# Two convolution channels summed in one PSUM bank, and a new order of the steps: a one-core diffusion layer

## The chip, the cores and the metric

The kernel runs on one core of a Trainium2 chip. The metric is the time of one execution on the device in microseconds (us); it comes as the median of several runs. One execution more is taken with a hardware profiler: its trace shows what each engine did and when. The engines are TensorE (PE; PEld is its weight load), VectorE (DVE), ScalarE (ACT), GpSimd (POOL) and SyncE (SP), which issues nearly all the transfers. Each runs its own instructions in the order in which they were written, and waits for the others by semaphores. SBUF is the large memory on the chip, PSUM the small one of eight banks into which TensorE writes.

## What is computed

One layer over 256 latent tokens of width 1024, with 256 context tokens, all in 32-bit floats. Cut to what matters here:

```python
mod   = silu(c) @ w_ada + b_ada                   # shifts, scales and gates, 6 x 1024 columns
z     = modulate(rms_norm(x)) @ w_in              # 2048 columns; for the context too
u     = z[:, :512] * sigmoid(z[:, 512:1024])      # 4 blocks of 128 channels ("ct")
u     = dwconv(u, conv_dw, 31 taps) + conv_b      # along rows of 64 tokens, each channel by itself
conv  = silu(layer_norm(u) * ln_g + ln_b)
lru   = scan(forward) + scan(backward)            # gated linear recurrence of z[:, 1024:1536]
lru   = lru * gelu(z[:, 1536:])
x     = x + g1 * (concat(conv, lru) @ w_out)
h     = modulate(rms_norm(x))
y     = top-1-group / top-2-expert mixture of 32 experts, (silu(h @ w1) * (h @ w3)) @ w2
out   = rms_norm(x + g2 * y) * final_g
```

The weights of the 32 experts are 12 MB each and are read whole; they make up most of the 443 MB that come from HBM.

## The kernel before

**Two parts.** The prelude computes all up to the router's choice of experts. The expert part (lines 826 and on) then runs expert by expert: `up` (line 828) loads a weight matrix in four tiles of 1 MB and multiplies each as it arrives. All weights go through a pool of 19 buffers of 1 MB (`slot()`, line 76). A buffer comes free when its last reader is done, and SP issues the transfers in program order, so a load waits until there is a buffer, and all loads behind it with it. PSUM tiles (`bank()`, line 73) come out of a pool of eight in the same way.

**The order of the prelude.** Up to line 345 it is written out: norm, modulation, and the projection for value and gate of the convolution (`vgproj`) in four stages of the contraction. The rest is the string `ORDER` (lines 30 to 40), a list of steps by one letter (line 807), each with its indices. The program's instructions are written in just this order; so it sets each engine's queue, and SP's and POOL's too. The steps that matter here:

- `v`, `l`: last stage of the value and gate projection, and the gating into a padded buffer `cbs[ct]` (lines 316 and 428). `glu` takes a tanh on ScalarE and a product on VectorE.
- `t` (`vtap`, line 444): a tap of the convolution on VectorE. It takes y = x * w + y with x a shifted view of `cbs[ct]` and y a quarter of `ypre`, both in SBUF, 256 columns; the first tap of a channel block (line 448) sets y, the other 30 (line 450) are chained. `VTAPS` gives 31 taps to VectorE for ct 0 and ct 3, none for ct 1, nine for ct 2, 71 in all.
- `s` and `i` (`stap`, line 452): the other 53 taps, of ct 1 and ct 2. The product x * w is made on ScalarE (`s`, line 467) or VectorE (`i`, line 465) into a ring of four buffers, and POOL adds it (line 468).
- `h`, `o`: the weights of the recurrent branch come in two buffers. Each is split into a rounded part (a cast, `split_hi`, line 287) and a rest (a subtract, `split_lo`, line 293), so that a product can be made of three passes in the format float32r. `HI` and `LO` name the engines: V, S or G (VectorE, ScalarE, POOL).
- `u`, `c`: the product of the recurrent branch for one block (line 361, 24 matmuls; the first half needs the first buffer's split alone), and its short convolution, one pass on ScalarE and three on VectorE that read the PSUM bank (lines 372 and 376).
- `p`, `a`, `d`, `q`, `n`: gate products into two banks (line 382), their activations on ScalarE with one square on the engine that `SQ` names (line 390), two products on VectorE (410, 411), a square root (414) and the scans (416).
- `b`: one of 16 steps of the modulation's remaining columns; it loads 1 MB and multiplies it (line 478). `z`, `e`: the gelu branch. `L`, `I`, `J`: load an output weight and split it; only the pair of blocks that `OS` marks is split, and `WH`, `WL`, `MH`, `ML` name the engines.
- `M`, `C`, `Q`, `R`, `N`: the layer norm of the convolution. `M` sums the four blocks on TensorE (line 558), and VectorE reads the mean (line 560).
- `X`, `O`, `D` and on: the output product, the residual, the second norm, the router and the gathering of tokens for the first experts.

Of the kernel before, what the change touches and what calls it, by code (L numbers as in the profile page):

```python
# [16 lines left out]
T = 256  # L17
# [10 lines left out]


ORDER = """  # L30
v0 h0 h1 o0 v1 l0 v3 o1 v2 t l1 l3 u1 i t*3 s u0 t*2 b t*2 s t b s t i l2 i t s*4 t*5 s t s t*3 i*2 t*3 s t*3 i
s*2 c1 t i t*2 b t b s i s*2 t*3 c0 b s*2 u2 t s*2 c2 i p10 p00 a10 i t a00 u3 p11 t i t i s t*3 p20 b p01 t i
t*2 s t d10 s i c3 t*2 i p30 t i s t b s i t*2 a20 i a30 t b r1 w t p21 t*2 s d00 a01 t i b t*2 s q10 d30 i t
d20 t i t*2 i*2 b*2 q20 s q30 t*4 i t q00 n00 z0 t z1 s p31 d01 L2 t*3 s L0 a21 t n20 a11 b k1 a31 I0 M C2 z2
n10 C1 C0 I2 C3 L4 b d21 d11 b d31 q21 q11 q01 Q b*2 R n01 z3 N1 N0 L6 e0 N2 N3 X3 X1 n30 n21 n11 X0 m0 J0 O001
e3 I4 X2 J2 O110 J4 O100 e1 q31 O011 O111 O112 x O000 e2 g I6 O003 X4 O012 n31 m3 O010 J6 m1 X5 O101 m2 X7 X6 r2
O105 O015 O002 O102 O103 O005 O007 O013 O006 O004 O016 O106 O113 O107 j k2 O017 O014 y O114 O104 O115 D00 D01
H00 Y0 O116 D10 O117 H01 H10 D11 K00 H11 B K01 Z0 K10 T0 K11 P0 F0 G02 G00 G06 G04 Y1 G05 T1 Z1 G07 P1 F1 G03 G01
G10 G11 G12 G16 G14 A1 U0 G15 U1 G17 G13 U2 U3 A0 U4 U7 U6 U5
"""  # L40
VTAPS = (31, 0, 9, 31)
SIDE = (1, 2,)
HI, LO = "VS", "VG"
SQ = ("SSSG", "SSSG")
LNSQ = "SGGG"
XC = ("SS", "SV")
WH, WL = "SSVS", "VGVV"
MH, ML = "GSSGGSVS", "GVGGGVVG"
GL = ("GG", "GG")
OS = "0010"  # L50


COLS = {}
# [9 lines left out]
def hybrid_layer(ctx: ExitStack, tc: tile.TileContext, sp_d, x_d, c_d, bada_d, rb_d, fg_d, gw_d,  # L63
# [103 lines left out]
    def first_norm(s, src):  # L167
        for t in range(2):
            S.activation(xn[:, 1], src[:, t], AF.Square, accum_out=sums[:, 2 * s + t:2 * s + t + 1])
        rstd_t = rsqrt_pow(sums[:, 2 * s:2 * s + 2], 2, 1.0 / D)  # L170
        for t in range(2):
            V.tensor_scalar(diag[:, 2 * s + t], ident, rstd_t[:, t:t + 1], None, OP.mult)
        for k2 in range(4):
            pt = bank()
            for i in range(4):
                k, t = k2 * 2 + i // 2, i % 2
                P.matmul(pt[:, i * 128:(i + 1) * 128], src[:, t, k * 128:(k + 1) * 128], diag[:, 2 * s + t],
                         start=True, stop=True)
            (V.tensor_copy, S.copy)[s](xs[s][:, k2 * 2:k2 * 2 + 2], pt.rearrange("p (k t) -> p k t", k=2))

    first_norm(0, x1)

# [104 lines left out]
    def split_hi(w, hi, lo, en):  # L287
        if en is S:
            S.copy(hi, w)  # L289
        else:  # L290
            en.tensor_copy(hi, w)

    def split_lo(w, hi, lo, en):
        en.tensor_tensor(lo, w, f(hi), OP.subtract)  # L294
# [31 lines left out]
    def prepare(q):  # L326
        ada_h(q, pt)
        for k in range(2 * q, 2 * q + 2):
            modulated(k)

    w = load_wz(0)
    split_hi(*w, S)
    split_lo(*w, G)
    prepare(0)
    for q in range(4):
        ks = range(2 * q, 2 * q + 2)
        if q < 3:
            w = load_wz(q + 1)
            rows = ada_rows(ada_first(q + 1))
            split_hi(*w, S)  # L340
            split_lo(*w, G)
            vgproj(0, ks)
            pt = ada_turn(rows)
            prepare(q + 1)
            for ct in range(1, 4):
                vgproj(ct, ks)
# [88 lines left out]
    def rows4(a):  # L435
        return a.rearrange("p (r t) -> p r t", r=4)

    vtaps = [(ct, j) for ct in range(4) for j in range(VTAPS[ct])]  # L440
    staps = [(ct, j) for ct in SIDE for j in range(VTAPS[ct], 31)]
    nring = [0]

    def vtap():
        ct, j = vtaps.pop(0)
        y, x, w = rows4(ypre[:, ct]), cbs[ct][:, :, j:j + 64], dwh[:, j * 4 + ct:j * 4 + ct + 1]
        if j == 0:
            V.tensor_scalar(y, x, w, col("convb", ct), OP.mult, OP.add)
        else:
            V.scalar_tensor_tensor(y, x, w, y, OP.mult, OP.add)  # L450

    def stap(vec=False):
        ct, j = staps.pop(0)
        n = VTAPS[ct]
        y, x, w = rows4(ypre[:, ct]), cbs[ct][:, :, j:j + 64], dwh[:, j * 4 + ct:j * 4 + ct + 1]
        acc = rows4(g2bc[:, 752:1008]) if n else y
        if j == 0:
            S.activation(acc, x, AF.Identity, scale=w, bias=col("convb", ct))
        elif j == n:
            S.mul(acc, x, w)  # L460
        else:
            p = rows4(fgbc[:, nring[0] % 4 * T:(nring[0] % 4 + 1) * T])
            nring[0] += 1
            if vec:
                V.tensor_scalar(p, x, w, None, OP.mult)  # L465
            else:
                S.mul(p, x, w)
            G.tensor_tensor(acc, acc, p, OP.add)  # L468
        if j == 30 and n:
            G.tensor_tensor(y, y, acc, OP.add)  # L470


    ada = {}
# [329 lines left out]
    def route(t):  # L803
        val["r", t] = topk(t)

    engines = {"V": V, "S": S, "G": G}
    steps = dict(v=lambda ct: vgproj(ct, (6, 7)), l=glu, t=vtap, s=stap, i=lambda: stap(True), u=u_mm, c=u_conv, p=gate_mm,
                 a=lambda ct, d: gate_act(ct, d, engines[SQ[d][ct]]), d=gate_v, q=root, n=scan, b=ada_step,
                 h=lambda i: split_hi(*wu[i], engines[HI[i]]), o=lambda i: split_lo(*wu[i], engines[LO[i]]),
# [376 lines left out]
```

## Time and profile before

| | us |
|---|---|
| median of 3 runs | 1161.3 (1160.74 to 1161.55) |
| the profiled execution's own time | 1162.45 |
| its span, first to last instruction | 1160.7 |
| TensorE busy in the span | 1022.5 (88%) |
| VectorE busy | 331.1 (29%) |
| ScalarE busy | 167.5 (14%) |
| POOL busy | 95.3 (8%) |
| bytes moved | 445.25 MB, a mean of 384 GB/s |

The profile gives start and length of each instruction, grouped by source line, operation and tile, and what ended a wait. Busy shares over the whole span say little here, because the prelude and the expert part have different limits; the views are read by stretches of time from the span's start.

### The profile page before, as it was taken

The page shows a single profiled execution, that of the slowest core. Times are in us where ns is not written, and L with a number is a line of the kernel's source. Part 1 is how long each engine was busy: PE and PEld are TensorE (multiplying, and loading weights), DVE is VectorE, ACT ScalarE, POOL GpSimd, SP SyncE. Part 2 cuts the span into 40 slices and gives each one's busy share as a digit, 9 for nine tenths or more (in the row PEclk, how much of TensorE's full clock was granted, in tenths as well). Part 3 has the DMA queues.
Part 4 walks back from the last instruction along what each step waited for, and adds up shares of the span by engine and source line. Part 5 has one row for each costly group of instructions (what it writes and reads, how often), then busy time and mean ns, then how long its engine had stood idle before and what let it go on. Part 6 is the DMA issues. An engine that isn't in the chain of part 4 may idle for free.

```text
span 1160.7 us, 12269 instructions
## 1 busy us (share of the span) xinstructions
PE 1022.5 (88%) x4923; PEld 425.1 (37%) x4923; DVE 331.1 (29%) x644; ACT 167.5 (14%) x313; POOL 95.3 (8%) x105
## 2 busy tenths in 40 slices
PE   7897899899999998988888888888888888888796
PEld 6763456443434232323232323232323222232234
DVE  4899993412121112111211111212121111111113
ACT  3436762300101000000000000000000000000002
POOL 2455522000000000000000000000000000000001
PEclk9898898899999999999999999999999999999999
DMA  9856869498999999999999999999999999999995
GB/s 346 300 195 240 327 262 389 183 423 348 420 419 420 421 420 419 419 420 420 420 420 421 419 419 420 419 420 419 420 419 420 420 420 419 419 420 420 419 393 190
DMA packets 76930, 445.25 MB, mean 384 GB/s; under 512 B 7187, under 2 KB 17475, under 8 KB 27204
## 3 DMA queue, kind: packets, MB, share of 16 engines
q1 hardware_dynamic: 76658, 443.85, 93.9%
q8 instruction: 41, 0.67, 0.2%
q10 hardware_dynamic: 210, 0.55, 0.1%
q14 instruction: 21, 0.17, 0.0%
HBM read 443.32 MB, written 1.05 MB: 383 GB/s over the span
## 4 chain that ended last, share of the span: by engine, by line
DMA 65%; PE 19%; DVE 13%; issue 1%; ACT 0%; POOL 0%; SPq 0%; DVEq 0%; ACTq 0%; POOLq 0%
DMA slot<-in_w_dram 65%; PE bank L835 12%; DVE xn L450 4%; PE bank L661 2%; PE bank L770 1%; PE bank L857 1%; DVE fgbc L465 1%; DVE slot L294 1%; PE bank L322 1%; DVE slot L376 1%; DVE slot L284 1%; DVE slot L410 1%; DVE slot L419 1%; DVE lw L209 0%; DVE slot L411 0%
## 5 line engine op out<-in xcount | busy, mean ns | idle before, releaser
L835 PE MATMUL bank<-slot 128*64 128x512 f32 x1984 | 469.4, 601 | 82.7 <-DMA slot<-in_w_dram 82.7
L835 PEld LDWEIGHTS bank<-slot 128*64 128x64 f32 x1984 | 129.4, 136 | 406.3 <-DMA slot<-in_w_dram 194.2
L835 PE MATMUL bank<-slot,gt 128*64 128x512 f32 x992 | 220.4, 596 | 3.6 <-DMA slot<-in_w_dram 2.6
L946 DVE TENSOR_TENSOR sl<-sl,bank 128x512 f32<-128x512 f32 x31 | 21.3, 687 | 491.7 <-issue 468.0
L835 PEld LDWEIGHTS bank<-slot,gt 128*64 128x64 f32 x992 | 68.1, 137 | 144.9 <-issue 133.0
L982 DVE TENSOR_TENSOR yy<-bank,g2bc 64x512 f32<-64x512 f32 x62 | 42.7, 688 | 194.6 <-PE bank L835 194.2
L939 ACT ACTIVATE sl<-bank 128x512 f32<-128x512 f32 x31 | 18.5, 597 | 456.8 <-PE bank L835 456.8
L1103 POOL TENSOR_TENSOR slot<-x,fgbc 128x256 f32<-128x256 f32 x6 | 4.2, 727 | 938.3 <-DVE x L1100 938.3
L857 PE MATMUL bank<-yy,st 128*128 128x512 f32 x120 | 58.0, 606 | 0.0
L770 PE MATMUL bank<-oh,xn 128*128 128x256 f32 x224 | 54.6, 387 | 0.0
L770 PEld LDWEIGHTS bank<-oh,xn 128*128 128x128 f32 x224 | 41.9, 197 | 14.7 <-issue 11.4
L966 ACT COPY gt<-bank 128x256 f32<-128x256 f32 x31 | 11.5, 373 | 221.4 <-DVE gt L965 221.4
L862 DVE TENSOR_TENSOR x<-x,bank 128x512 f32<-128x512 f32 x60 | 39.7, 683 | 7.1 <-PE bank L857 7.1
L776 ACT ACTIVATE slot<-bank,gsp 128x256 f32<-128x256 f32 x32 | 18.0, 564 | 152.4 <-PE bank L770 148.9
L322 PE MATMUL bank<-slot 128*128 128x256 f32 x192 | 28.8, 310 | 6.0 <-ACT slot L283 4.8
L857 PEld LDWEIGHTS bank<-yy,st 128*128 128x128 f32 x120 | 20.6, 191 | 26.5 <-issue 23.2
L322 PEld LDWEIGHTS bank<-slot 128*128 128x128 f32 x192 | 26.6, 212 | 8.1 <-ACT slot L283 5.8
L779 DVE TENSOR_SCALAR slot<-bank,gsp 128x256 f32<-128x256 f32 x32 | 17.3, 543 | 41.1 <-ACT slot L776 41.0
L294 POOL TENSOR_TENSOR slot<-slot 128x2048 fp32r<-128x2048 f32 x5 | 23.8, 4768 | 26.9 <-ACT slot L289 26.9
L450 DVE SCALAR_TENSOR_TENSOR xn<-cb,sp,xn 128x256 f32<-128x256 f32 x38 | 25.1, 662 | 0.7
L468 POOL TENSOR_TENSOR xn<-xn,fgbc 128x256 f32<-128x256 f32 x30 | 23.7, 791 | 16.6 <-DVE fgbc L465 9.6
L367 PE MATMUL bank<-slot 128*128 128x512 f32 x96 | 23.4, 400 | 1.4 <-DVE slot L294 1.4
(246 smaller groups left out, 706.7 us busy)
## 6 DMA issues: line engine op xcount, KB each, us to landing
slot<-in_w_dram SPq DMA_DIRECT2D x372, 1024.0 KB, 19.9
slot<-in_wada_dram SPq DMA_DIRECT2D x16, 1024.0 KB, 6.7
slot<-in_w_dram SPq DMA_DIRECT2D x24, 512.0 KB, 10.8
slot<-in_wada_dram SPq DMA_DIRECT2D x16, 512.0 KB, 10.8
slot<-in_win_dram SPq DMA_DIRECT2D x8, 1024.0 KB, 10.5
slot<-in_wout_dram SPq DMA_DIRECT2D x4, 1024.0 KB, 9.4
x<-in_x_dram SPq DMA_DIRECT2D x2, 512.0 KB, 4.3
slot<-in_ctx_dram SPq DMA_DIRECT2D x2, 512.0 KB, 6.6
```

Source lines behind the costliest of these rows:

```text
L294: en.tensor_tensor(lo, w, f(hi), OP.subtract)
L322: P.matmul(pvg[ct][:, i * T:(i + 1) * T], wz[k // 2][wi][:, k % 2, c:c + 128], x[k // 4][:, k % 4, 0:T], start=k + i + n == 0, stop=k == 7 ...
L367: P.matmul(pu, w, x[k // 4][:, k % 4], start=k + n == 0, stop=k == 7 and n == 2)
L450: V.scalar_tensor_tensor(y, x, w, y, OP.mult, OP.add)
L468: G.tensor_tensor(acc, acc, p, OP.add)
L661: P.matmul(p, m[:, q], w[:, c:c + 512], start=first and n == 0, stop=len(done) == 8 and n == len(passes) - 1)
L770: P.matmul(pg[:, i * 256:(i + 1) * 256], xn[:, t, pair(k)], oh[:, t].rearrange("p e s -> p (e s)"), start=t + i == 0, stop=t == 1 and i == ...
L835: P.matmul(ps[64 * h:64 * h + 64, :], xs(k2 * 2 + i), w[:, i, h * 512:(h + 1) * 512], start=k2 + i == 0, stop=k2 * 2 + i == 7, tile_positi ...
L857: P.matmul(pz, st[:, t * 128:(t + 1) * 128], yy[:, h * 512:(h + 1) * 512], start=True, stop=True)
L862: V.tensor_tensor(x1[:, t, q], x1[:, t, q], pz, OP.add)
L946: V.tensor_tensor(gg, sl, pb, OP.mult)
L982: V.tensor_tensor(yy[o:o + 64, h * 512:(h + 1) * 512], py[64 * h:64 * h + 64, :], g2bc[64 * h:64 * h + 64, h * 512:(h + 1) * 512], OP.mult)
```

## The change

Three things. The sums of the blocks ct 0 and ct 3 (`PC`) stand in the two halves of one PSUM bank, and only the last tap writes the result to `ypre` in SBUF. The string `ORDER` is a new one; with it 11 steps `i` stand where there were 24, the rest are `s`. And some splits go to other engines: both casts and both subtracts of the recurrent branch's weights (`HI`, `LO`) to ScalarE and POOL, three gate squares, and the subtract of the output weight (`WL`, third letter) to POOL. `ZH`, `ZL` and `FN` are new names for choices that were fixed.

```diff
--- before.py
+++ after.py
@@ -28,26 +28,30 @@
 
 
 ORDER = """
-v0 h0 h1 o0 v1 l0 v3 o1 v2 t l1 l3 u1 i t*3 s u0 t*2 b t*2 s t b s t i l2 i t s*4 t*5 s t s t*3 i*2 t*3 s t*3 i
-s*2 c1 t i t*2 b t b s i s*2 t*3 c0 b s*2 u2 t s*2 c2 i p10 p00 a10 i t a00 u3 p11 t i t i s t*3 p20 b p01 t i
-t*2 s t d10 s i c3 t*2 i p30 t i s t b s i t*2 a20 i a30 t b r1 w t p21 t*2 s d00 a01 t i b t*2 s q10 d30 i t
-d20 t i t*2 i*2 b*2 q20 s q30 t*4 i t q00 n00 z0 t z1 s p31 d01 L2 t*3 s L0 a21 t n20 a11 b k1 a31 I0 M C2 z2
-n10 C1 C0 I2 C3 L4 b d21 d11 b d31 q21 q11 q01 Q b*2 R n01 z3 N1 N0 L6 e0 N2 N3 X3 X1 n30 n21 n11 X0 m0 J0 O001
-e3 I4 X2 J2 O110 J4 O100 e1 q31 O011 O111 O112 x O000 e2 g I6 O003 X4 O012 n31 m3 O010 J6 m1 X5 O101 m2 X7 X6 r2
-O105 O015 O002 O102 O103 O005 O007 O013 O006 O004 O016 O106 O113 O107 j k2 O017 O014 y O114 O104 O115 D00 D01
-H00 Y0 O116 D10 O117 H01 H10 D11 K00 H11 B K01 Z0 K10 T0 K11 P0 F0 G02 G00 G06 G04 Y1 G05 T1 Z1 G07 P1 F1 G03 G01
-G10 G11 G12 G16 G14 A1 U0 G15 U1 G17 G13 U2 U3 A0 U4 U7 U6 U5
+v0 v1 h0 h1 o0 l0 t*2 v3 o1 t*3 v2 u0 l3 t*2 l1 l2 u1 t*2 b t s t s t*2 b t s t*2 s t s*3 t s*2 t s t i t s t s*2 t i
+t*2 c1 t*2 b t s*2 t*3 s*2 t s b s*3 t*2 c0 b s*2 u2 s c2 s p10 s i p00 b a10 t*2 i*3 a00 u3 t p11 t s t w i t*3 b p01
+t p20 s c3 s t s t s p30 t*2 d10 s t s*2 i t*2 a20 s*2 a30 t b t d00 t p21 a01 t r1 b t*2 s q10 t d30 i t d20 i b s b
+t*2 s L0 q30 s q20 t s t*3 q00 z0 t L4 t b z1 t i p31 t*2 n00 s t*2 n20 d01 M a11 a31 k1 I0 C2 L2 z2 n10 C1 a21 I2 C0
+C3 d21 d11 b q21 q11 q01 d31 Q z3 b R n01 e0 N1 L6 N2 x X1 N0 b X2 N3 I4 X3 b n30 n11 X0 m0 J0 J2 O001 e3 O002 J4 O100
+q31 O111 O102 O112 O000 O011 e1 O012 I6 O010 O003 g n21 n31 O110 e2 O113 J6 j m1 X5 O101 m3 m2 X4 X7 X6 r2 O103 O005
+O007 O013 O006 O105 O004 O015 O106 k2 O016 O114 O104 O017 O014 O107 D00 O115 D01 y H00 Y0 D10 O117 O116 H01 H10 D11
+K00 H11 K01 Z0 K10 K11 T0 P0 F0 G06 B G04 G02 G00 Y1 T1 G07 P1 Z1 G03 F1 G01 G05 G10 G11 G12 G16 G14 A1 U0 G17 G15 U1
+U4 G13 U2 U3 U6 U5 A0 U7
 """
 VTAPS = (31, 0, 9, 31)
+
+PC = (0, 3)
 SIDE = (1, 2,)
-HI, LO = "VS", "VG"
-SQ = ("SSSG", "SSSG")
+HI, LO = "SS", "GG"
+SQ = ("SGGG", "SSSS")
 LNSQ = "SGGG"
 XC = ("SS", "SV")
-WH, WL = "SSVS", "VGVV"
-MH, ML = "GSSGGSVS", "GVGGGVVG"
+WH, WL = "VSVS", "VVGV"
+MH, ML = "VSSGGSSG", "GVGGGVVG"
 GL = ("GG", "GG")
 OS = "0010"
+ZH, ZL = "SSSS", "GGGG"
+FN = "VS"
 
 
 COLS = {}
@@ -176,7 +180,7 @@
                 k, t = k2 * 2 + i // 2, i % 2
                 P.matmul(pt[:, i * 128:(i + 1) * 128], src[:, t, k * 128:(k + 1) * 128], diag[:, 2 * s + t],
                          start=True, stop=True)
-            (V.tensor_copy, S.copy)[s](xs[s][:, k2 * 2:k2 * 2 + 2], pt.rearrange("p (k t) -> p k t", k=2))
+            (V.tensor_copy if FN[s] == "V" else S.copy)(xs[s][:, k2 * 2:k2 * 2 + 2], pt.rearrange("p (k t) -> p k t", k=2))
 
     first_norm(0, x1)
 
@@ -328,17 +332,18 @@
         for k in range(2 * q, 2 * q + 2):
             modulated(k)
 
+    engines = {"V": V, "S": S, "G": G}
     w = load_wz(0)
-    split_hi(*w, S)
-    split_lo(*w, G)
+    split_hi(*w, engines[ZH[0]])
+    split_lo(*w, engines[ZL[0]])
     prepare(0)
     for q in range(4):
         ks = range(2 * q, 2 * q + 2)
         if q < 3:
             w = load_wz(q + 1)
             rows = ada_rows(ada_first(q + 1))
-            split_hi(*w, S)
-            split_lo(*w, G)
+            split_hi(*w, engines[ZH[q + 1]])
+            split_lo(*w, engines[ZL[q + 1]])
             vgproj(0, ks)
             pt = ada_turn(rows)
             prepare(q + 1)
@@ -437,17 +442,26 @@
 
 
 
+    yps = {}
+
+    def ypart(ct):
+        if ct not in yps:
+            b = bank()
+            for i, c in enumerate(PC):
+                yps[c] = b[:, i * T:(i + 1) * T]
+        return yps[ct]
+
     vtaps = [(ct, j) for ct in range(4) for j in range(VTAPS[ct])]
     staps = [(ct, j) for ct in SIDE for j in range(VTAPS[ct], 31)]
     nring = [0]
 
     def vtap():
         ct, j = vtaps.pop(0)
-        y, x, w = rows4(ypre[:, ct]), cbs[ct][:, :, j:j + 64], dwh[:, j * 4 + ct:j * 4 + ct + 1]
+        y, x, w = rows4(ypart(ct) if ct in PC else ypre[:, ct]), cbs[ct][:, :, j:j + 64], dwh[:, j * 4 + ct:j * 4 + ct + 1]
         if j == 0:
             V.tensor_scalar(y, x, w, col("convb", ct), OP.mult, OP.add)
         else:
-            V.scalar_tensor_tensor(y, x, w, y, OP.mult, OP.add)
+            V.scalar_tensor_tensor(rows4(ypre[:, ct]) if j == 30 else y, x, w, y, OP.mult, OP.add)
 
     def stap(vec=False):
         ct, j = staps.pop(0)
@@ -467,7 +481,7 @@
                 S.mul(p, x, w)
             G.tensor_tensor(acc, acc, p, OP.add)
         if j == 30 and n:
-            G.tensor_tensor(y, y, acc, OP.add)
+            (V.tensor_tensor(y, acc, rows4(ypart(ct)), OP.add) if ct in PC else G.tensor_tensor(y, y, acc, OP.add))
 
 
     ada = {}
@@ -803,7 +817,6 @@
     def route(t):
         val["r", t] = topk(t)
 
-    engines = {"V": V, "S": S, "G": G}
     steps = dict(v=lambda ct: vgproj(ct, (6, 7)), l=glu, t=vtap, s=stap, i=lambda: stap(True), u=u_mm, c=u_conv, p=gate_mm,
                  a=lambda ct, d: gate_act(ct, d, engines[SQ[d][ct]]), d=gate_v, q=root, n=scan, b=ada_step,
                  h=lambda i: split_hi(*wu[i], engines[HI[i]]), o=lambda i: split_lo(*wu[i], engines[LO[i]]),
```

## Rows read from the trace of the kernel before

**Rows 1.** Stretches ahead of the expert products: us, busy by engine, clock, DMA share, GB/s.
```profile
203.00:206.00 3.00, 1.46 (x6) 1.35 (x7) 2.03 (x11) 2.56 (x4) 0.94 (x2) 0.50 0.02 5
...
219.00:222.00 3.00, 3.00 (x16) 0.87 (x12) 0.44 (x2) 0.38 (x1) 0.00 (x0) 1.00 0.99 396
```

**Rows 2.** The chain of waits, 225 to 420 us: start, length, what.
```profile
381.43 19.89 DMA slot<-in_w_dram
```

**Rows 3.** The stretch of the convolution, columns as in rows 1.
```profile
69.00:145.00 76.00, 63.62 (x329) 35.49 (x328) 74.08 (x124) 46.49 (x78) 43.28 (x53) 0.91 0.62 244
```

**Rows 4.** VectorE by line and form, 60 to 175 us: busy us, mean ns.
```profile
L450 DVE SCALAR_TENSOR_TENSOR xn<-g2bc,sp,xn 128x256 f32<-128x256 f32 x30 | 19.8, 661 | 0.9
...
L465 DVE TENSOR_SCALAR fgbc<-cb,sp 128x256 f32<-128x256 f32 x12 | 5.5, 463 | 0.0
```

**Rows 5.** VectorE in order of time: start, length, instructions.
```profile
62.17 6.58 DVE L294 TENSOR_TENSOR slot<-slot 128x2048 fp32r<-128x2048 f32 x1
...
69.12 0.41 DVE L448 TENSOR_SCALAR xn<-g2bc,sp 128x256 f32<-128x256 f32 x1
...
120.60 3.40 DVE L450 SCALAR_TENSOR_TENSOR xn<-cb,sp,xn 128x256 f32<-128x256 f32 x4
...
142.80 2.04 DVE L450 SCALAR_TENSOR_TENSOR xn<-cb,sp,xn 128x256 f32<-128x256 f32 x4
...
147.75 0.41 DVE L560 TENSOR_SCALAR cb<-bank 128x256 f32<-128x256 f32 x1
...
169.04 2.29 DVE L294 TENSOR_TENSOR slot<-slot 128x2048 fp32r<-128x2048 f32 x1
```

**Rows 6.** VectorE's instructions on a PSUM bank: min/median/max ns.
```profile
L376 DVE SCALAR_TENSOR_TENSOR slot<-bank,sp,slot x12: 732/748/749, 89.7 to 113.9; 128x510 f32<-128x510 f32 x8, 128x508 f32<-128x508 f32 x4
L582 DVE TENSOR_TENSOR xn<-xn,bank x4: 411/414/415, 158.8 to 159.8; 128x256 f32<-128x256 f32 x4
```

**Rows 7.** VectorE by line and form, 189 to 197 us: the residual.
```profile
L675 DVE TENSOR_TENSOR x<-x,t 128x512 f32<-128x512 f32 x4 | 2.8, 692 | 0.1
L674 DVE TENSOR_TENSOR t<-bank,fgbc 128x512 f32<-128x512 f32 x4 | 2.8, 688 | 1.5 <-PE bank L661 1.4
```

**Rows 8.** POOL in order of time.
```profile
52.49 4.60 POOL L294 TENSOR_TENSOR slot<-slot 128x2048 fp32r<-128x2048 f32 x1 [3.33 <-ACT slot L289]
61.09 5.51 POOL L294 TENSOR_TENSOR slot<-slot 128x2048 fp32r<-128x2048 f32 x1 [4.00 <-ACT slot L289]
...
89.89 2.35 POOL L468 TENSOR_TENSOR xn<-xn,fgbc 128x256 f32<-128x256 f32 x3 [2.25 <-DVE fgbc L465]
```

**Rows 9.** ScalarE in order of time: a cast of 2048 columns.
```profile
59.12 1.89 ACT L289 CAST slot<-slot 128x2048 fp32r<-128x2048 f32 x1
```

**Rows 10.** ScalarE by line and form, 60 to 175 us: one of a gate's activations.
```profile
L398 ACT ACTIVATE slot<-t,nkh 128x512 f32<-128x512 f32 x8 | 6.5, 814 | 0.3
```

**Rows 11.** TensorE in order of time, with the wait ahead in brackets.
```profile
68.80 10.76 PE L367 MATMUL bank<-slot 128*128 128x512 f32 x46 [1.35 <-DVE slot L294]
...
109.53 3.65 PE L387 MATMUL bank<-slot 64*64 64x512 f32 x16
...
117.69 1.92 PE L492 MATMUL bank<-slot,silc 128*32 128x512 f32 x16
...
121.40 1.52 PE L486 MATMUL bank<-bada,ident 48*32 48x128 f32 x16
...
125.57 7.17 PE L306 MATMUL bank<-slot 128*128 128x256 f32 x32
...
175.68 3.03 PE L661 MATMUL bank<-slot,t 128*128 128x512 f32 x6 [2.06 <-ACT t L289]
...
214.44 7.09 PE L835 MATMUL bank<-slot 128*64 128x512 f32 x32
```

**Rows 12.** POOL by line and form, 60 to 175 us: adds of channel 2.
```profile
L468 POOL TENSOR_TENSOR g2bc<-g2bc,fgbc 128x256 f32<-128x256 f32 x21 | 17.4, 830 | 14.9 <-DVE fgbc L465 14.1
```

**Rows 13.** TensorE by line and form, 60 to 200 us: the mean product M.
```profile
L558 PE MATMUL bank<-xn,ones 128*128 128x256 f32 x8 | 4.1, 672 | 3.5 <-ACT slot L404 2.1 <-DVE xn L450 1.4
```

## The prediction

> **What bounds the kernel now.** I read the stretches of the DMA first, then the chain of waits, then the busy times by stage, then each engine in order of time inside the stage that counts.
>
> The chain of waits, as I followed it, lies on TensorE's expert products to 381 us and then goes from one weight transfer to the next [rows 2]. But already from 219 us the DMA engines are 0.99 busy [rows 1], and the products before 381 us use up what they bring. So from there the end is a fixed number of bytes at a fixed rate: it moves with the moment at which this stream starts. It starts when the first expert products hand buffers back (they begin at 214.4 us [rows 11]); just before, from 203 us on, the DMA does nothing (share 0.02, 5 GB/s) [rows 1], because all weight buffers are full and wait for the router. A prelude that is shorter by X moves the start, and so the end, by X.
>
> The prelude's middle, 69 to 145 us, is VectorE's: 74.08 of 76 us busy, against 46.5 on ScalarE and 43.3 on POOL; TensorE shows 63.6 [rows 3]. That is the stage of the 31-tap convolution. VectorE's 68 chained taps there take 0.66 us each and the 23 tap products that it makes for POOL 0.46 [rows 4]. But a tap runs in 0.51 us while POOL is idle (142.8 us, four in 2.04) and in 0.85 while POOL is busy (120.6 us, four in 3.40) [rows 5]. So a third of a tap's time is POOL in the way. After the stage a shorter one follows on VectorE; then the output products on TensorE, with one gap of 2.06 us at 175.7 us [rows 11]; then the router, which the change leaves as it is.
>
> **The change, part by part.**
>
> *Taps in PSUM (channels 0 and 3).* 60 chained taps get one SBUF operand in place of two. What the trace has of such a form is the mix-in of the short convolution (line 376: input in PSUM, sum in SBUF): 12 of them from 89.7 to 114.7 us, 732 to 749 ns [rows 6], some inside POOL's work (89.9 to 92.2 us [rows 8]), the last with POOL idle. So one SBUF operand isn't slowed by POOL. The Trainium skill says the same (SBUF — State Buffer, Who interferes with whom). No row has VectorE writing PSUM. Bounds for a tap: 0.41 us (256 columns out of PSUM, line 582) below, 0.75 us (line 376, twice the columns) above [rows 6]. I take 0.51, the same chained instruction without POOL: 60 x (0.66 - 0.51) = 9.0 us off VectorE. The ends give 15 us, and a loss of 5.
>
> *The splits of the input weights (h0, o0).* VectorE loses a cast and a subtract of 6.58 us; the same subtract takes 2.29 us at 169.0 us, where POOL is idle [rows 5]: at 62.2 us it ran against POOL's own of 5.51 us, which takes 4.60 alone [rows 8]. In the new order ScalarE casts both (1.89 each [rows 9]) before the first tanh of the gating: 59.1 + 3.8 = 62.9, and with that tanh and the first gating product (0.4 each) the first tap starts at 63.7 in place of 69.1 [rows 5]: 5.4 us. POOL subtracts both, 61.0 to 65.6 and 65.6 to 70.2. TensorE can run half of the first recurrent-branch product (u0) on the first of them; it ends that and u1 (46 instructions in 10.76 us [rows 11], so 5.6 a product) at 70.2 + 2.8 + 5.6 = 78.6, where before it ended at 79.6. Who waits is c1 on VectorE: with 25 taps and five short instructions ahead of it, it could start at 78.1 and starts at 79.4, behind ScalarE's pass over the product (512 columns, 0.8 [rows 10]): 1.3 us lost.
>
> *Tap products.* VectorE makes 10 in place of 23. 13 x 0.46 are 6.0 us, of which I take 4.9, as the records of neighbours overlap a little. ScalarE takes them at some 0.5 each (half the columns of [rows 10]), 6.5 us onto its 46.5 [rows 3], in a stage that gets to be 63: 10 us are free. POOL adds 51 products at no more than 0.83 [rows 12]: 70.2 + 42 + 3 for one more square than before is 116, ahead of the last tap. The two squares that POOL gets and the one that it gives are in this. All of it costs nothing as long as ScalarE and POOL keep that lead of about 10 us; beyond it every us counts.
>
> *New waits.* c2 waits for u2. TensorE's order is u1, five ada steps (0.96 each, their bias 1.52 [rows 11]), u2: 78.6 + 6.3 + 5.6 = 90.5, and ScalarE's pass 91.3. VectorE arrives at 79.4 + 2.3 for c1 + 3.1 for six taps in PSUM + 2.3 for three in SBUF + 2.3 for c0 = 89.4 and loses 1.9. Behind c2 on VectorE stand the rest of channel 2's taps and those of channel 3. One gate step (d01, two instructions of the length in [rows 7], 1.4) goes behind the last tap.
>
> VectorE's last tap, which ended at 144.8 [rows 5]: 5.4 + 9.0 + 4.9 + 1.4 - 1.3 - 1.9 = 17.5 earlier, 127.3.
>
> *TensorE is late next.* From u2 on: two gate pairs (1.83 each) and an ada step, 95.2; u3, 100.8; then six gate pairs 11.0, six ada steps 5.8, bias 1.5, two gelu products 7.2 (32 in 7.17) [rows 11]: 126.3 without a wait. But the sums hold one of eight PSUM banks for all that time, and gate pairs take two each until ScalarE has read them. Counted through the order, live banks reach 10 at p30 in place of 9, so p30 and the second ada bank wait for a release: bounds 0 and one gate's activations each (four or five of up to 0.81 [rows 10], so 3 us). I take 1.5 each: 129.3. The mean product M stands behind these; its eight matmuls are 4.1 us [rows 13], 133.4, and VectorE's use of it (line 560) comes 14.3 us before its 147.75 [rows 5].
>
> The strings FN, ZH, ZL and MH change no instruction: they name the engines of before, or splits that this kernel doesn't make.
>
> *After M* the steps on VectorE are the old ones in another order, and ScalarE reloads its tables once less: 0. The subtract of the fourth split (2.29 us, 169.0) leaves VectorE for POOL and runs earlier, against scans that it will slow; it stood ahead of the last scan, for which TensorE waited 2.06 us [rows 11]. Between nothing and 2.06 I take 1.0.
>
> *SP's queue.* Two loads of the output weights (L0, L4) move ahead of the twelfth ada load and L6 ahead of the last two; three of the last four ada steps stand later in TensorE's order, and their buffers, which the first expert weights get, come free later by that. The 13 us in which the DMA stands idle before the first expert product [rows 1] cover this; without them each us late would count in full.
>
> Sum: 14.3 + 1.0 = 15.3. The profiled execution took 1162.45 for a span of 1160.7; less 15.3 that is 1147.1. The median of the runs lies 1.1 lower: **1146 us**.
>
> **The rivals.**
>
> *PSUM taps cost a fixed sum more.* A chained line 376 has 0.748 us for about 510 columns [rows 6], while two 512-column rows with and without a PSUM input are equal, 688 and 692 ns (lines 674, 675) [rows 7]. The first leaves room for some 0.06 a tap, the second speaks against it: 60 x 0.06 = 3.6 less, 1150. Against the change speaks also a table of the Trainium skill (VectorE: DVE Perf Modes, the errata section), with a fixed 120 cycles for PSUM sources and 58 for SBUF. By it, an estimate, 65 ns a tap and 1150. The equal rows disagree with that. Chance 0.12.
>
> *Banks and handoffs are the new bound.* Four gate or ada steps (p30, p21, b9, p31) each wait a whole gate of activations, 3 us: 12 in place of my 3, M 9 later, 1155. For it: live banks pass eight, and TensorE is within 3 us of VectorE. Against it: ScalarE has 10 us free in the stage, so a gate that is ready is read soon. Chance 0.15.
>
> *Slower.* Writing and rereading PSUM in place costs VectorE much more. The taps' 9.0 and the 6.3 of the rest go when a tap takes 0.51 + 15.3/60 = 0.765, just past the upper bound. At the 0.85 of a hindered tap [rows 5] 20.4 us are lost against my sum: 1166. For it: no row of the form at all. Against: half the columns of line 376. Chance 0.07.
>
> *The change doesn't reach the end.* The expert weights come so much later that the DMA idles as long as before: 1161. Against it the 13 idle us. Chance 0.05.
>
> **How the numbers follow.** The forecast (14 to 20 us of VectorE time, of which TensorE lets 10 to 19 through: 1142 to 1151) has 0.61. A measurement of this kernel tells about 0.2%, 2.3 us, from no change. Faster: 0.61 + 0.12 + 0.15, so 0.88; same 0.05; slower 0.07. The range of 8 in 10 takes in the forecast, the fixed sum and most of the bank case, with the taps' lower bound below: 1139 to 1156.
>
> **What would show it.** Right: taps of channels 0 and 3 near 0.5 us whether POOL is busy or not; the first tap near 64, u1's end near 79, the last tap near 127, line 560 near 133, the first expert product 15 us earlier; DMA still idle ahead of it. Wrong: taps over 0.6 us; VectorE idle for long at c1 or c2; TensorE waiting for gate activations; no idle DMA before the first expert product, or an end that moves by less than that product does.

## The result, and the profile of the changed kernel

The changed kernel takes 1142.4 us (median of 4 runs, 1140.06 to 1145.41), the kernel before 1161.4 (4 runs): ratio 0.9838 (95%: 0.9813 to 0.9862), 19.1 us less. Two executions far off all others, one of the kernel before with 3573 us and one of e8_norm_rows_first with 2050 us, are left out of the figures. The forecast had 1146 with a range of 1139 to 1156: faster, as it said, and by about 4 us more than its sum. The profiled execution took 1141.62 for a span of 1139.8, so it lies 20.9 us below the span of before.

VectorE in the convolution, grouped by line and form (columns as in [rows 4]); lines have moved by 14, so a chained tap is line 464:

```profile
L464 DVE SCALAR_TENSOR_TENSOR bank<-g2bc,sp,bank 128x256 f32<-128x256 f32 x29 | 14.1, 488 | 0.8
L464 DVE SCALAR_TENSOR_TENSOR bank<-cb,sp,bank 128x256 f32<-128x256 f32 x29 | 14.1, 486 | 0.7
L464 DVE SCALAR_TENSOR_TENSOR xn<-cb,sp,xn 128x256 f32<-128x256 f32 x8 | 5.9, 734 | 0.2
L479 DVE TENSOR_SCALAR fgbc<-g2bc,sp 128x256 f32<-128x256 f32 x5 | 3.6, 732 | 1.2 <-POOL xn L482 1.2
L479 DVE TENSOR_SCALAR fgbc<-cb,sp 128x256 f32<-128x256 f32 x5 | 2.2, 440 | 0.0
```

A tap whose sum stands in PSUM takes 487 ns; before it took 661 [rows 4]. The eight taps of channel block 2, whose sum is still in SBUF, take 734 in the same stretch. VectorE in order of time (start, length, the wait ahead in brackets):

```profile
63.49 0.55 DVE L462 TENSOR_SCALAR bank<-g2bc,sp 128x256 f32<-128x256 f32 x1
67.95 6.78 DVE L464 SCALAR_TENSOR_TENSOR bank<-g2bc,sp,bank 128x256 f32<-128x256 f32 x13
78.31 0.92 DVE L479 TENSOR_SCALAR fgbc<-g2bc,sp 128x256 f32<-128x256 f32 x1 [0.90 <-POOL xn L482]
90.65 2.31 DVE L381 SCALAR_TENSOR_TENSOR slot<-bank,sp,slot 128x508 f32<-128x508 f32 x3 [0.85 <-ACT slot L377]
111.88 2.58 DVE L464 SCALAR_TENSOR_TENSOR bank<-cb,sp,bank 128x256 f32<-128x256 f32 x5
127.23 0.48 DVE L464 SCALAR_TENSOR_TENSOR xn<-cb,sp,bank 128x256 f32<-128x256 f32 x1
130.93 0.41 DVE L574 TENSOR_SCALAR cb<-bank 128x256 f32<-128x256 f32 x1
147.59 4.88 DVE L426 TENSOR_TENSOR_SCAN slot<-slot 128x256 f32<-128x256 f32 x1
```

The first tap is at 63.5, the last ends at 127.7, and VectorE reads the mean at 130.9; in [rows 5] these are 69.1, 144.8 and 147.75. POOL, in order of time, over the first of these taps and at their end:

```profile
60.99 9.20 POOL L298 TENSOR_TENSOR slot<-slot 128x2048 fp32r<-128x2048 f32 x2 [4.00 <-ACT slot L293]
70.15 20.46 POOL L482 TENSOR_TENSOR xn<-xn,fgbc 128x256 f32<-128x256 f32 x25
...
116.66 6.28 POOL L482 TENSOR_TENSOR g2bc<-g2bc,fgbc 128x256 f32<-128x256 f32 x7 [3.81 <-ACT fgbc L481]
...
125.28 0.99 POOL L484 TENSOR_TENSOR xn<-xn,g2bc 128x256 f32<-128x256 f32 x1
```

Thirteen taps run in 6.78 us, 0.52 each, from 67.95, first under POOL's long subtract and then under its adds, with no difference. From 112.85 to 116.66 POOL is idle; the five taps from 111.88, the last three of them in that gap, take 0.52 each as well. TensorE in order of time, the lines that answer to [rows 11] and the work before the router:

```profile
70.25 8.00 PE L372 MATMUL bank<-slot 128*128 128x512 f32 x34 [0.18 <-POOL slot L298]
108.68 1.07 PE L392 MATMUL bank<-slot 64*64 64x512 f32 x4 [1.19 <-ACT slot L409]
112.32 1.07 PE L392 MATMUL bank<-slot 64*64 64x512 f32 x4 [0.57 <-ACT slot L409]
127.77 1.99 PE L572 MATMUL bank<-xn,ones 128*128 128x256 f32 x8
137.27 5.39 PE L310 MATMUL bank<-slot 128*128 128x256 f32 x16
146.70 9.71 PE L675 MATMUL bank<-slot,xn 128*128 128x512 f32 x22
173.97 1.88 PE L675 MATMUL bank<-slot,xn 128*128 128x512 f32 x4
193.84 7.09 PE L848 MATMUL bank<-slot 128*64 128x512 f32 x32
```

The first expert product (line 848) begins 20.6 us earlier. The stretches ahead of it, as in [rows 1], still show an idle DMA, for some 9 us where it was 13:

```profile
186.00:190.00 4.00, 4.00 (x25) 3.75 (x25) 2.13 (x12) 3.06 (x6) 0.99 (x1) 0.50 0.34 137
190.00:194.00 4.00, 4.00 (x23) 3.87 (x24) 2.46 (x10) 2.28 (x6) 1.57 (x2) 0.62 0.00 0
```

**Where the 20.6 us come from**, by stages of the two traces:

| stage | before | after | gained |
|---|---|---|---|
| start to the first tap | 69.1 | 63.5 | 5.6 |
| first tap to VectorE's use of M | 78.6 | 67.4 | 11.2 |
| from there to the first output product | 14.05 | 15.8 | -1.7 |
| output products, first to last | 34.1 | 29.15 | 5.0 |
| from there to the first expert product | 18.5 | 18.0 | 0.5 |
| first expert product to the end of the span | 946.3 | 946.0 | 0.3 |

The fourth row is what the forecast missed. Output products of before, the same columns by stretches: the wait of [rows 11] and what follows it.

```profile
173.60:175.70 2.10, 0.04 (x2) 0.02 (x1) 0.09 (x2) 0.48 (x2) 1.91 (x3) 1.00 1.02 429
175.70:178.50 2.80, 2.77 (x6) 1.98 (x7) 0.45 (x1) 0.41 (x1) 0.17 (x1) 0.58 1.00 418
178.50:182.30 3.80, 3.80 (x10) 1.96 (x9) 0.00 (x0) 0.00 (x0) 0.00 (x0) 0.86 1.02 425
```

TensorE waits at 1.00 (the 2.4 GHz level), and when it goes on, the granted clock is 0.58 and then 0.86, part of the time at 1.2 GHz. By these clocks the same work at 1.00 would have been (1 - 0.58) x 2.8 + (1 - 0.86) x 3.8 = 1.7 us shorter, an estimate. The changed kernel has no such wait: the whole stretch of its output products is at 1.00.

```profile
146.70:176.00 29.30, 29.30 (x93) 15.21 (x90) 18.13 (x22) 9.88 (x19) 11.41 (x12) 1.00 1.00 413
```

### The profile page after: what moved, and what is told of

It reads as the page before. It is cut to its first block, busy times and chain, and to the rows that moved or that the text cites. A ratio compares the mean times of both kernels' runs of the same rounds, so it can differ in the third digit from the quotient of the medians.

```text
span 1139.8 us, 12269 instructions
## 1 busy us (share of the span) xinstructions
PE 1015.8 (89%) x4923; PEld 420.9 (37%) x4923; DVE 309.8 (27%) x628; ACT 172.7 (15%) x325; POOL 103.0 (9%) x108
## 4 chain that ended last, share of the span: by engine, by line
DMA 68%; PE 22%; DVE 6%; issue 1%; ACT 1%; POOL 1%; SPq 0%; DVEq 0%; ACTq 0%; POOLq 0%
DMA slot<-in_w_dram 68%; PE bank L848 11%; PE bank L675 2%; PE bank L372 2%; DVE bank L464 1%; PE bank L870 1%; PE bank L784 1%; PE bank L326 1%; PE bank L506 1%; DVE slot L288 1%; PE bank L810 1%; DVE lw L213 0%; PE bank L310 0%; DVE g1s L268 0%; POOL slot L298 0%
## 5 line engine op out<-in xcount | busy, mean ns | idle before, releaser
L848 PEld LDWEIGHTS bank<-slot,gt 128*64 128x64 f32 x992 | 68.1, 137 | 144.8 <-issue 133.0
L952 ACT ACTIVATE sl<-bank 128x512 f32<-128x512 f32 x31 | 18.5, 597 | 456.6 <-PE bank L848 456.6
L298 POOL TENSOR_TENSOR slot<-slot 128x2048 fp32r<-128x2048 f32 x7 | 32.4, 4631 | 31.0 <-ACT slot L293 23.5
L870 PEld LDWEIGHTS bank<-yy,st 128*128 128x128 f32 x120 | 20.6, 191 | 26.5 <-issue 23.2
L976 PEld LDWEIGHTS bank<-ident,sl 128*128 128x128 f32 x124 | 19.4, 201 | 11.1 <-issue 7.1
## 6 DMA issues: line engine op xcount, KB each, us to landing
slot<-in_wout_dram SPq DMA_DIRECT2D x4, 1024.0 KB, 10.4
```

The lines of the kernel that those rows point to most:

```text
L848: P.matmul(ps[64 * h:64 * h + 64, :], xs(k2 * 2 + i), w[:, i, h * 512:(h + 1) * 512], start=k2 + i == 0, stop=k2 * 2 + i == 7, tile_positi ...
L870: P.matmul(pz, st[:, t * 128:(t + 1) * 128], yy[:, h * 512:(h + 1) * 512], start=True, stop=True)
L976: P.transpose(pt[:, j * 128:(j + 1) * 128], gg[:, pair(j)], ident)
```

## The experiments

The theory: (a) the sums in PSUM, and nothing else in the change, make taps as fast as with POOL idle; (b) the new order and the splits let that reach the first expert product, by having no wait among the output products; (c) from there the end follows. Rivals: the order alone or the splits alone do it; the held bank costs; the products moved to ScalarE are the gain. Kernels are named by what they do; ratios are to the kernel before, with 95% intervals.

The work ahead of the taps, which no edit touches, ends at another time in each execution: VectorE's last operation of the modulation (line 285 before, 289 after) starts between 58.9 and 63.3 us. The last four columns are therefore counted from that operation: to the first tap, to VectorE's use of M, the length of the output products from first to last, and to the first expert product, all in us.

| kernel | median | ratio | first tap | M | outputs | first expert product |
|---|---|---|---|---|---|---|
| before (profiled) | 1161.4 | | 8.5 | 87.2 | 34.1 | 153.9 |
| after (profiled) | 1142.4 | 0.9838 (0.9813 to 0.9862) | 3.0 | 70.5 | 29.2 | 133.4 |
| e0_changed (after again) | 1141.8 | 0.9836 (0.9814 to 0.9859) | 3.0 | 70.5 | 29.2 | 131.6 |
| e1_sums_in_sbuf | 1159.6 | 0.9976 (0.9960 to 0.9992) | 3.0 | 87.5 | 29.1 | 151.9 |
| e2_only_psum_sums | 1154.0 | 0.9925 (0.9903 to 0.9946) | 8.5 | 77.5 | 34.2 | 144.7 |
| e3_splits_back | 1145.6 | 0.9854 (0.9837 to 0.9870) | 8.5 | 74.6 | 29.1 | 135.3 |
| e4_products_as_before | 1144.0 | 0.9842 (0.9823 to 0.9861) | 3.0 | 74.5 | 29.2 | 135.8 |
| e5_wo_rest_on_v | 1143.7 | 0.9837 (0.9820 to 0.9853) | 3.0 | 70.4 | 29.2 | 133.4 |
| e6_two_banks | 1141.8 | 0.9823 (0.9804 to 0.9842) | 3.0 | 70.4 | 29.2 | 133.4 |
| e7_old_order | 1153.3 | 0.9923 (0.9901 to 0.9945) | 3.0 | 74.6 | 36.8 | 144.5 |
| e8_norm_rows_first | 1144.8 | 0.9855 (0.9838 to 0.9872) | 3.0 | 70.4 | 29.2 | 134.0 |
| e9_before_no_gap | 1159.7 | 0.9974 (0.9963 to 0.9985) | 8.5 | 87.1 | 29.9 | 150.1 |
| e10_rows_first_late_ada | 1143.9 | 0.9845 (0.9825 to 0.9865) | 3.0 | 70.4 | 31.5 | 134.5 |
| e11_old_order_no_gap | 1146.6 | 0.9861 (0.9839 to 0.9882) | 3.0 | 74.7 | 29.9 | 137.7 |

In all of them the span ends 945.9 to 947.1 us after the first expert product starts. So (c) holds, and the last column tells what an edit is worth, to some 2 us: the changed kernel itself stands there with 133.4 and with 131.6.

**e1_sums_in_sbuf**: the changed kernel with the sums in SBUF.

```diff
-PC = (0, 3)
+PC = ()
```

> The changed kernel with the sums of channels 0 and 3 back in SBUF (PC empty), all else as changed. If POOL in the way of VectorE's second SBUF operand is what the change takes away: these 60 taps go from 0.51 us to 0.66 or more, since POOL is now busier (0.85 if always hindered), the last tap comes 9 to 20 us later than 127.7, and the time is 1150 to 1160. If the PSUM bank costs more in waits than the taps give (gate products waiting for a bank): TensorE's waits of 1.8 us at the gate products go and the time is 1140 to 1143.

It took 1159.6; the sums in PSUM are worth some 16 us in the new order (0.9976 against 0.9838; M 17.0 later), and the order and the splits without them some 3. VectorE in order of time, and by line:

```profile
64.52 2.28 DVE L462 TENSOR_SCALAR xn<-g2bc,sp 128x256 f32<-128x256 f32 x1
66.84 4.68 DVE L464 SCALAR_TENSOR_TENSOR xn<-g2bc,sp,xn 128x256 f32<-128x256 f32 x1
71.55 1.52 DVE L464 SCALAR_TENSOR_TENSOR xn<-g2bc,sp,xn 128x256 f32<-128x256 f32 x3
...
L464 DVE SCALAR_TENSOR_TENSOR xn<-g2bc,sp,xn 128x256 f32<-128x256 f32 x30 | 25.3, 843 | 0.9
L464 DVE SCALAR_TENSOR_TENSOR xn<-cb,sp,xn 128x256 f32<-128x256 f32 x38 | 26.0, 684 | 1.0
```

and POOL beside the first two taps:

```profile
62.02 4.62 POOL L298 TENSOR_TENSOR slot<-slot 128x2048 fp32r<-128x2048 f32 x1 [4.00 <-ACT slot L293]
66.61 4.63 POOL L298 TENSOR_TENSOR slot<-slot 128x2048 fp32r<-128x2048 f32 x1
```

With the sum in SBUF, a tap that meets a subtract of POOL ends only with it: the first tap ends at 66.80, POOL's first subtract at 66.64; the second tap takes 4.68 us to 71.52, POOL's second subtract ends at 71.24; the three behind it, with POOL idle, take 0.51 each. In the changed kernel no tap under these subtracts takes more than 0.55. Block 0 averages 843 ns here, more than the 661 of before. The two held taps lose some 6 us, about the 5.6 by which the first tap starts earlier. So, by this count, both splits on POOL pay only because the sums have left SBUF; no run moves the splits alone.

**e2_only_psum_sums**: the kernel before with the new `ypart`, `vtap` and `PC`, and nothing else.

```diff
+PC = (0, 3)
-y, x, w = rows4(ypre[:, ct]), ...
+y, x, w = rows4(ypart(ct) if ct in PC else ypre[:, ct]), ...
-V.scalar_tensor_tensor(y, x, w, y, OP.mult, OP.add)
+V.scalar_tensor_tensor(rows4(ypre[:, ct]) if j == 30 else y, x, w, y, OP.mult, OP.add)
```

> The kernel before with nothing but the sums of channels 0 and 3 in one PSUM bank, in the old order and with the old splits. If the taps gain by themselves: 60 taps at 0.51 in place of 0.66, the last tap 6 to 9 us earlier than 144.8, time 1152 to 1156. If the old order can't use it, because VectorE then waits at c1, c0 and c2 for TensorE and ScalarE, or banks run short: 1159 to 1162.

It took 1154.0, 8 us less. The taps are those of the changed kernel to 3 ns (488 and 483), M is 9.7 earlier, and the wait of 2.06 us among the output products stands as before, in TensorE's order of time:

```profile
167.27 2.75 PE L671 MATMUL bank<-slot,t 128*128 128x512 f32 x6 [2.06 <-ACT t L290]
```

**e7_old_order**: the changed kernel with the `ORDER` of before (so PSUM sums, splits and squares in the old order).

> The changed kernel with the old order of the steps; sums, splits and squares as changed. If the sums and the splits carry the gain and the order only arranges it: 1147 to 1153. If the order is what brings the gain: 1157 or more.

It took 1153.3, within the intervals the time of e2, although M is 2.9 earlier (74.6 for 77.5). By stretches, TensorE waiting among its output products:

```profile
160.70:164.70 4.00, 0.09 (x1) 0.00 (x0) 1.55 (x3) 0.45 (x2) 3.92 (x6) 0.86 1.01 420
164.70:167.50 2.80, 2.79 (x6) 2.11 (x7) 0.48 (x1) 0.44 (x1) 0.20 (x1) 0.50 1.01 421
167.50:171.10 3.60, 3.60 (x7) 1.54 (x6) 0.00 (x0) 0.00 (x0) 0.00 (x0) 0.60 1.00 416
```

The subtract of the output weight (`J4`), now on POOL, takes 4.83 us from 155.89, and VectorE's last scan, 1.22 us in the kernel before, is held under it:

```profile
156.39 5.42 DVE L429 TENSOR_TENSOR_SCAN slot<-slot 128x512 f32<-128x512 f32 x1
```

TensorE's wait, which stands behind this scan, is 3.92 us, the clock behind it 0.50 and 0.60, and the output products take 36.8 us. What the splits gain at the start is lost here. The order is worth some 10 us on top (0.9923 against 0.9838).

**e9_before_no_gap**: the kernel before with the split of the output weight (`I4`, `J4`) behind the last scan, and the products that don't need a split ahead of those that do.

```diff
-... e3 I4 X2 J2 O110 J4 O100 ... n31 m3 ... r2 O105 O015 O002 O102 O103 O005 O007 O013 ...
+... e3 X2 J2 O110 O100 ... n31 I4 J4 m3 ... r2 O002 O102 O103 O013 O105 O015 O005 O007 ...
```

> The kernel before with the split of the output weight (I4, J4) moved behind the last scan, and four plain output products moved ahead of the first split one, so that TensorE doesn't wait 2.06 us at 173.6 us. If the wait costs itself and then the clock (0.58 and 0.86 in the 6.6 us after it, some 1.7 us): TensorE's output products end 3 to 4 us earlier, 1157 to 1158.5. If it costs its length alone: 1159 to 1160. If something else holds the end: 1161.

The time fell by 3.0 us (0.9963 to 0.9985 of before, so 1.7 to 4.3). By stretches, TensorE is busy all through the output products:

```profile
163.00:178.00 15.00, 15.00 (x55) 6.52 (x53) 12.68 (x13) 10.16 (x16) 7.98 (x6) 1.00 1.01 419
178.00:193.00 15.00, 15.00 (x55) 9.04 (x54) 4.20 (x7) 2.59 (x7) 2.93 (x6) 1.00 1.01 421
```

They take 29.9 us in place of 34.1: a wait of 2.06 us was worth 4.2, with the clock at 1.00 throughout. The first expert product gains 3.8 of it. That is the profile; the interval of the runs does not tell 4.2 from the wait's length alone.

**e11_old_order_no_gap**: e7 with the two moves of e9 and that subtract back on VectorE (`WL`, third letter).

> The changed kernel with the old order, the fourth split's subtract on VectorE again and behind the last scan, and the plain output products ahead of the split ones, so that TensorE has no wait among the output products. With the old order as it was it waited 3.92 us there and lost some 2 more by the clock after it. If that is what the old order gave away: 1147 to 1149. If the old order loses in the convolution's stage alone: 1151 to 1154.

1146.6; by stretches, the output products:

```profile
148.00:162.00 14.00, 14.00 (x54) 6.43 (x53) 13.02 (x14) 10.17 (x15) 6.83 (x5) 1.00 1.01 414
162.00:180.00 18.00, 18.00 (x71) 11.01 (x69) 5.72 (x10) 4.57 (x11) 4.08 (x8) 1.00 1.02 422
```

M stays where e7 has it, and the first expert product comes 6.8 earlier, for a wait of 3.92; the medians say 6.7 (1153.3 and 1146.6), and the closest two runs lie 5.4 apart, so here the runs, too, say that the wait cost more than its length. So of the 11.1 us between e7 and the changed kernel (144.5 and 133.4) 6.8 are the missing wait, and some 4 are the order of the convolution's stage (M 74.7 and 70.5).

**e3_splits_back**: the two splits of the input weights on the engines of before.

```diff
-HI, LO = "SS", "GG"
+HI, LO = "VS", "VG"
```

> The changed kernel with the recurrent branch's weight splits back where they were (first cast and first subtract on VectorE). If VectorE's own work still sets M: the first tap at about 69.5 in place of 63.5, of which the waits at c1 and c2 (some 2 us) take a part back, M and the first expert product 3 to 4 us later, 1145 to 1147. If TensorE's order sets M (in the changed kernel M follows the last gate pair without a wait): 1142 to 1143, as changed.

1145.6, 1 to 2 us more than e5 and e10 beside it (0.9837 and 0.9845); the intervals overlap. The first tap is 5.5 us later, M 4.1, the first expert product 1.9 later than in the changed kernel's profile and 3.7 later than in e0_changed. So some 2 to 4 us, of which the runs show the smaller end.

**e4_products_as_before**: 13 of the steps `s` are `i` again.

> The changed kernel with 13 of the tap products back on VectorE, at the places (counted in products) where the old order had them. If VectorE's sum sets M: 13 products of 0.26 to 0.7 us, M and the time 3 to 5 us later, 1145 to 1147. If ScalarE and POOL had become the pace, so that VectorE has time: 1141 to 1143.

1144.0. M is 4.0 us later, and TensorE, with all its work ahead of M done, waits for the taps:

```profile
132.82 2.70 PE L572 MATMUL bank<-xn,ones 128*128 128x256 f32 x8 [3.34 <-DVE xn L464]
```

The first expert product is 2.4 later than in the changed kernel's profile and 4.2 later than in e0_changed; the runs (0.9842 against 0.9836 beside it; medians 1144.0 and 1141.8) show 1 to 2, with intervals that overlap. The profile says which way it goes, the timing does not settle the size.

**e5_wo_rest_on_v**: the subtract of the output weight's split (`J4`) on VectorE in the new order.

```diff
-WL = "VVGV"
+WL = "VGVV"
```

> The changed kernel with the subtract of the output weight's split back on VectorE (2.3 us). On POOL it holds up one scan (4.88 us at 147.6 in place of 0.7). If TensorE's plain output products cover either: 1141.5 to 1143.5, no change. If the held scan is on the path: 2 us less, 1140.

No difference, as expected: in the new order this subtract lies where nothing waits for it. VectorE's scan beside it takes

```profile
147.74 0.69 DVE L426 TENSOR_TENSOR_SCAN slot<-slot 128x256 f32<-128x256 f32 x1
```

where it took 4.88 at 147.59 in the changed kernel, under POOL's subtract; the output products start and end within 0.2 us of it all the same.

**e6_two_banks**: a whole bank for each of the two blocks.

```diff
-            b = bank()
             for i, c in enumerate(PC):
-                yps[c] = b[:, i * T:(i + 1) * T]
+                yps[c] = bank()[:, i * T:(i + 1) * T]
```

> The changed kernel with the sums of the two channels in a bank each, so that one bank more is held through the taps. If a gate that is ready is read soon, so that the missing bank costs little: TensorE's waits at the gate products rise from 1.8 us by 1 to 3, the time by 0 to 2, 1142 to 1144. If banks are the bound that the rival names, three or four waits of 3 us: 1149 to 1155.

1141.8 against 1141.8 for e0_changed. The two gate waits on TensorE did not rise as I had expected; they are those of the changed kernel:

```profile
107.15 1.08 PE L392 MATMUL bank<-slot 64*64 64x512 f32 x4 [1.19 <-ACT slot L409]
...
110.80 1.08 PE L392 MATMUL bank<-slot 64*64 64x512 f32 x4 [0.57 <-ACT slot L409]
```

**e8_norm_rows_first** and **e10_rows_first_late_ada** tried to win back the 1.7 us between M and the output products: the layer norm's rows (`Q`, `R`) ahead of the last gates, and in e10 also two ada steps among the output products.

```diff
-C3 d21 d11 b q21 q11 q01 d31 Q z3 b R n01 e0 N1 ...
+C3 d21 Q d11 b R q21 q11 q01 d31 z3 b n01 e0 N1 ...
```

> The changed kernel with the norm's variance (Q) read behind the first gate step and its rows (R) written ahead of the last gelu product, so that the normalisation (N) doesn't wait 2.3 us for TensorE. If the start of the output products is the path: TensorE begins them some 2 us earlier, the first expert product too, 1140 to 1141. If the ada steps and the router row ahead of them hold TensorE anyway: 1142 to 1143.

> As the one before, and the last two ada steps behind the first output products. If the start of the output products is the path: 3 to 4 us earlier than in the changed kernel, 1138 to 1140. If the later release of the two ada buffers delays the first expert weights by more than the idle time of the DMA (10 us in the changed kernel) covers: 1142 or more.

Neither gained (1144.8 and 1143.9). In e8 VectorE no longer waits at the norm, but TensorE does, and the output products start 87.4 us behind the modulation's last operation (86.2 in the changed kernel):

```profile
134.02 1.98 PE L588 MATMUL bank<-ones,g2bc 128*128 128x1 f32 x16 [1.78 <-ACT g2bc L580]
137.41 1.22 PE L161 MATMUL bank<-ident,r 128*128 128x128 f32 x4 [0.41 <-POOL r L155]
138.42 4.64 PE L310 MATMUL bank<-slot 128*128 128x256 f32 x16
```

In e10 they start 85.7 behind it and take 31.5 us, two ada steps among them. I had taken VectorE's wait of 2.31 us at the norm for the cause; but TensorE, busy from M to the output products but for 0.8 us, sets their start.

**e0_changed**: the changed kernel again, beside e4, e6 and e11.

> The changed kernel itself once more, beside the next three on the same chip: 1141 to 1144.

0.9836, as the first time. Its last gelu product, in TensorE's order of time, is faster:

```profile
137.00 3.70 PE L310 MATMUL bank<-slot 128*128 128x256 f32 x16
```

That is 3.70 in place of 5.39, with a granted clock of 1.00 in place of 0.74 from 137 to 143.5 us; M to the first output product is then 14.1, as before the change. So the third stage's 1.7 us do not always come with the change: the product ran below 2.4 GHz in one execution and not in the other. With the same code there, e5 and e6 also have 15.8 from M to the output products, e3 has 14.1; the five kernels with the old order have 14.1 to 14.3. Why the clock falls in some executions and not in others, no run tells.

## Why the forecast was right, and where it was short

**The frame** held. The DMA is idle ahead of the first expert product in both kernels, and the span ends 946 to 947 us after that product in all profiles. The rival that the change does not reach the end falls with it.

**Taps.** Forecast 9.0 us off VectorE at 0.51 each; measured 60 x (0.661 - 0.487) = 10.4. The forecast's 0.51 was the step from one tap to the next and its 0.66 the length of a record; a record of an unhindered tap in SBUF is 0.48 too, so the mechanism is right and the term a little small. They take the same time whether POOL is busy or not, which was the reason given. The Trainium skill says the same of an instruction of VectorE with at most one SBUF input (SBUF — State Buffer, Who interferes with whom), and the 13 taps in 6.78 us under POOL agree. The fixed sum that PSUM would cost and the slower tap both fall. By the table of the Trainium skill (VectorE: DVE Perf Modes, the errata section), an estimate, a tap would have been some 65 ns longer; no row shows that.

**First tap.** 5.4 forecast, 5.6 measured; u1 ended at 78.25 for 78.6.

**Products.** 4.9 forecast; VectorE's product time went from 10.5 to 5.8 us. In e4 M comes 4.0 later; how much of that reaches the end lies between 1 and 4. The lead of 10 us that POOL was to keep was not there: its last add ended at 126.3 in place of 116, 1.4 ahead of the last tap, after it had waited 3.81 us for a product of ScalarE. It cost nothing, but that was close.

**New waits.** 3.2 forecast at c1 and c2; measured 2.7, in four pieces (0.30, 0.90, 0.85, 0.61). Only the third, at c2, is where I put it. In the first two VectorE waits for POOL to free the ring of products, ahead of c1; the fourth is at c3. The last tap ended 17.1 us earlier (forecast 17.5).

**TensorE late next.** Forecast 3.0 us of waits for banks and 4.1 for M's matmuls. Measured 1.19 + 0.57, with one bank or two (e6), and 1.99: TensorE came to M from work, at 1.00, where before it had waited; the last tap had ended at 127.71 and M began at 127.77, so the two engines arrive there together. M's use came 16.8 earlier, not 14.3. Both terms were too dear by 3.3 us together; 1.2 of it went between M's end (129.8) and VectorE's use of it (130.9), which I had counted at nothing. The rival of banks and handoffs falls: in place of its four waits of 3 us there are two of 1.76 together, and a second held bank adds nothing (e6). What the first one costs, no run shows alone.

**The gap among the output products: the term that was mis-sized.** "Between nothing and 2.06 I take 1.0": it measured 5.0. The wait is gone, 2.06; the clock that it had lowered, about 2 (4.2 less 2.06 in e9, 1.7 by the rows above; in the three profiles with this wait, before, e2 and e7, the clock fell among these products, in the other eleven it stayed at 1.00); and a product of one row for the router (step `x`, 0.75) no longer stands among them. e9 shows the first two alone, 4.2. The bound of 2.06 was the wrong one, since it took the length of the wait for its price; [rows 11] gave the six matmuls behind it 3.03 us, and their clock was in the trace.

**After M: 0** held in e0_changed; the profiled execution lost 1.7 to the clock, as e5 and e6 did.

**SP's queue.** The remark has L0 wrong: it stood ahead of the twelfth ada load before, too, beside L2. Nothing hangs on it, as the DMA still idles.

By stages the errors are +0.2, +2.3, -1.7, +4.0 and +0.5, in all 5.3 us to the first expert product on the trace. Against the medians the forecast was 3.6 off: it took the median 1.1 below the profiled execution, and it lies 0.7 above.

By parts: the sums in PSUM give 8 us alone and 16 in the new order, where two long subtracts lie on POOL beside the taps; order and splits without them give some 3; the order gives some 10 with them, 6.8 of these by the missing wait; the splits nothing in the old order, 1 to 4 in the new one. The parts do not add; each makes room for the next. No kernel was measurably faster than the changed one.

## What to carry to other kernels

Where VectorE chains an accumulation in SBUF beside a busy POOL, put the accumulator in PSUM: it was 487 ns for 661 here, and it allows long POOL work beside it that would otherwise hold the chain. Price a wait of TensorE by the granted clock of the stretch behind it as well as by its own length: 2.06 us were worth 4.2. Read that clock in the trace, for it does not fall behind every wait. A local gain must be followed to the wait that takes it back: e7 reached the mean 2.9 us earlier than e2 and ended at the same time.

## What was unexpected of the hardware

A short wait can cost TensorE more than itself: with the wait of 2.06 us came a granted clock of 0.58 and 0.86 over the 6.6 us behind it, with that of 3.92 us 0.50 and 0.60 over 6.4. But others of nearly that length cost their length alone. In e11 TensorE waits 1.65, 1.82 and 1.72 us between 102 and 162 us, and the clock is 1.00 all through:

```profile
127.22 1.08 PE L391 MATMUL bank<-slot 64*64 64x512 f32 x4 [1.82 <-ACT t L401]
144.98 0.71 PE L160 MATMUL bank<-ident,r 128*128 128x128 f32 x4 [1.72 <-POOL r L154]
102.00:162.00 60.00, 52.48 (x282) 27.08 (x281) 58.11 (x94) 44.02 (x65) 29.69 (x32) 1.00 0.82 324
```

POOL does not slow VectorE's SBUF taps evenly, it holds them. In the kernel before 32 of the 68 chained taps start while an instruction of POOL runs; each ends 0.28 to 0.29 us behind that instruction (one 0.42), however long that one still had. So long operations of POOL cost far more than short ones. In e1 one tap took 4.68 us under a subtract of 4.63, and one 2.28, against 0.85 under POOL's adds of some 0.8 [rows 5]; a scan took 4.88 us in place of 0.69, and in e7 one took 5.42 in place of 1.22.

The first tap, unchained, is slower with its output in PSUM: 0.55 us against 0.41 into SBUF [rows 5]. The Trainium skill has PSUM operands in a slower mode (VectorE: DVE Perf Modes, Why PSUM operands drop a tier), and the two rows agree in direction. The chained taps show no such cost.

Executions of the changed kernel spread over 5 us (1140.7 to 1145.8 in e0_changed), and the profiles show two places: the clock at the last gelu product (1.7 us), and the work ahead of the first tap, which started its last modulation operation between 58.9 and 63.3 us (e10, e3).
